# Six matmuls over zeros behind the weights' transposes, and one group of products moved, in a Winograd convolution

## The chip, the cores and the metric

The kernel runs on one core of a Trainium2 chip. The metric is the device time of one execution in microseconds (us); lower is better. Before the change three runs took 126.02 us in the median, from 125.92 to 126.29.

## The reference

```
batch, c_in, h, w, c_out = 16, 64, 64, 64, 128
x_pad = np.pad(x, ((0, 0), (0, 0), (1, 1), (1, 1)), mode='constant')
for b, co, ci, kh, kw:
    output[b, co] += weight[co, ci, kh, kw] * x_pad[b, ci, kh:kh+h, kw:kw+w]
```

It is a 3x3 convolution with zero padding of 16 images of 64 channels and 64x64 pixels to 128 channels, all in float32.

## The kernel before

The images are taken in eight pairs, p = 0 to 7. The 64 channels of two images fill the 128 partitions, so that a product of an image is a matmul over 64 rows, and the two images' matmuls stand side by side (`b2`). Each pair is worked in two halves of 32 output rows, h = 0 and 1: sixteen halves in all.

The convolution is done by Winograd's method along the rows of the image: two neighbouring output rows are made from sums, differences and outer differences of input rows with transformed weights (`G0`, `G1`, `G2`, `G01`, `G21`, and `HP` and `HM`, which are half sums). In each half, sixteen row pairs are split in two blocks of eight: the F block is done by Winograd, the G block by another way of combining. A half has four accumulators in PSUM: `pf1`, `pg1`, `pf2` and `pg2`.

**Weights.** They are loaded as they lie (`w_raw`), cast to float16 by POOL and ACT (lines 84 and 85), and transposed on TensorE by nine matmuls against an identity (line 101), three for each kernel row kh in the order 0, 2, 1. Each kernel row has a tile of two PSUM banks, of which the first bank is used. From these, ACT and DVE make the transformed weights (lines 147 to 158). DVE's string is `th` (149), `HP` (150), the first sums `ss` (112), `HM` (153), the first differences `dd` (119), `G01` (156), `G21` (158) and the first outer differences `ee` (130). `th` reads the transposes of kh = 2.

**The loop.** For each half, POOL prepares sums, differences and outer differences two halves ahead (line 230; DVE makes those of the very first half itself), and ACT casts a part of the input (line 140). TensorE then runs seven groups of products through `mms` (line 178), in the order of the text: `pf1` from sums with `HP`, `pg1` from sums with `G1`, `pf2` from differences with `HM`, `pg2` from the cast input with `G01` and `G2`, and then the second parts: `pf1` from outer differences (`ee`) with `G0`, `pg1` from the cast input, `pf2` from `ee` with `G2`. ACT copies the first parts out (lines 245, 247, 249), and DVE and ACT put the halves together (lines 260 to 263): `g1` from `pg2`, `f0` from `pf1`, `f1` from `pf2`, `g0` from `pg1`.

**Order.** `keep` holds nearly every instruction in the order in which it is written, on each engine. PSUM has room for four tiles of two banks; a half's tile takes the room of whichever tile was given back first.

**Memory and transfers.** Eleven slots of SBUF (`homes`) hold both inputs and outputs: an output takes the slot of an input that is no longer wanted (`X_HOME`, `O_HOME`). Slot 6 is a spare at the start and holds the weights' intermediate values. All loads are issued by SyncE at the start, on one queue: first the weights, then nine transfers of x. The stores follow on the same queue. The first two are issued in the half (2, 0), behind line 262: an upper half of an image of pair 2, and an image of pair 0:

```
        if (p, h) == (2, 0):
            store(2, 1, 0, 32)
            store(0, 0)
```

Of the kernel before, what the change touches and what calls it, by code (L numbers as in the profile page):

```python
# [8 lines left out]
F32 = mybir.dt.float32  # L9
F16 = mybir.dt.float16  # L10
# [5 lines left out]
def kernel(  # L16
# [12 lines left out]
    nc = tc.nc  # L29
    B, CI, H, W = x.shape  # L30
    CO = weight.shape[0]
# [4 lines left out]
    keep = tc.keep_in_program_order  # L36
# [4 lines left out]
    psum = ctx.enter_context(tc.tile_pool(name="psum", bufs=4, space=bass.MemoryType.PSUM))  # L41
# [13 lines left out]
    def out_homes(p):  # L55
        lo, hi = O_HOME[p]
        return homes[:, lo : hi + 1 : hi - lo, :, :]
# [4 lines left out]
    def spared(at, n):  # L62
        return spare[:, at : at + n]
# [4 lines left out]
    def load(p, cuts=((0, H),)):  # L68
        for lo, hi in cuts:
            keep(  # L70
                nc.sync.dma_start(
                    xs[p][:, lo:hi, :], x_rows[128 * p : 128 * p + 128, lo:hi, :]
                )
            )

    load(0, ((0, 34), (34, H)))
    for p in range(1, NP):
        load(p)

    ident = spared(1920, 64).bitcast(F16)  # L80
    make_identity(nc, ident)

# [4 lines left out]
    G0, G1, G2, G21, G01, HP, HM = range(7)  # L87
# [7 lines left out]

    wps = {}
    for kh in (1, 0, 2):
        wps[kh] = psum.tile([128, 2, 512], F32, tag="acc", name="wp")[:, 0, 0 : 3 * CO]
    for kh in (0, 2, 1):
        for k in range(3):  # L100
            keep(nc.tensor.matmul(wps[kh][:, k * CO : k * CO + CO], w16[:, :, 3 * kh + k :: 9], ident))  # L101


    F_BLK, G_BLK = (1, 2), (0, 3)
# [33 lines left out]
    def cast(p, h):  # L138
        t = cpool.tile([128, 17, W], F16, tag="xh", name="xh")
        keep(nc.scalar.copy(t, xs[p][:, C_ROW[h] : C_ROW[h] + 17, :]))  # L140
        return t

    def transforms(eng, p, h):
        return sums(eng, p, h), diffs(eng, p, h), outers(eng, p, h)
# [17 lines left out]
    def mms(tiles, terms, start, stop):  # L162
        n = 3 * len(terms)
        i = 0
        for wi, src, row in terms:
            for kw in (1, 0, 2):
                c_lo, c_hi = max(0, 1 - kw), min(W, W + 1 - kw)
                lo, hi = 0, RB
                at, step, rows = row
                while at + step * lo < 0:  # L170
                    lo += 1
                while at + step * (hi - 1) > rows - 1:
                    hi -= 1
                first, last = at + step * lo, at + step * (hi - 1)
                for b2 in range(2):
                    p0 = 64 * b2
                    keep(
                        nc.tensor.matmul(  # L178
                            tiles[:, b2, lo:hi, c_lo:c_hi],
                            Wt[p0 : p0 + 64, wi, kw, :],  # L180
                            src[
                                p0 : p0 + 64,
                                first : last + 1 : step,
                                c_lo + kw - 1 : c_hi + kw - 1,
                            ],
                            start=start and i == 0,
                            stop=stop and i == n - 1,
                            skip_group_check=not start,
                        )
                    )  # L190
                i += 1

    def acc():
        return psum.tile([128, 2, RB, W], F32, tag="acc", name="acc")
# [3 lines left out]
    def store(p, b2, lo=0, hi=H, c=0, n=CO, eng=nc.sync):  # L198
        keep(
            eng.dma_start(  # L200
                out[2 * p + b2, c : c + n, lo:hi, :], out_homes(p)[c : c + n, b2, lo:hi, :]
            )
        )
# [9 lines left out]
    def stores(p, h):  # L213
# [3 lines that stand above are left out]
        elif (p, h) == (2, 1):  # L217
            store(2, 1, 32, H)
            store(0, 1)
            store_both(1)  # L220
            store(2, 0)
        elif (p, h) == (5, 1):
            store(5, 0)
            store(5, 1, 0, FEW)
        elif p > 2 and h == 1:
            store_both(p)

    for n, (p, h) in enumerate(halves):
        if n + 2 < len(halves):
            tr[halves[n + 2]] = transforms(nc.gpsimd, *halves[n + 2])  # L230
        if h == 0:
            both = out_homes(p)
            ov = both.rearrange("p b (j i) c -> p b j i c", i=2)
        ss, dd, ee = tr.pop((p, h))
        xc = xh.pop((p, h))
        jf, jg = RB * F_BLK[h], RB * G_BLK[h]
        sf, sg = jf - 16 * h, jg - 16 * h
        g_at = 2 * jg - C_ROW[h]


        f0, f1 = (ov[:, :, jf : jf + RB, i, :] for i in range(2))
        g0, g1 = (ov[:, :, jg : jg + RB, i, :] for i in range(2))
        pf1, pg1, pf2, pg2 = acc(), acc(), acc(), acc()
        mms(pf1, [(HP, ss, (sf, 1, 16))], True, True)
        keep(nc.scalar.copy(f1, pf1))  # L245
        mms(pg1, [(G1, ss, (sg, 1, 16))], True, True)
        keep(nc.scalar.copy(g1, pg1))  # L247
        mms(pf2, [(HM, dd, (0, 1, RB))], True, True)
        keep(nc.scalar.copy(f0, pf2))  # L249
        if (p, h) == (6, 0):  # L250

            store(5, 1, FEW, H, 0, 124, nc.scalar)
            store(5, 1, FEW, H, 124, 4, nc.scalar)
        if n + 1 < len(halves):
            xh[halves[n + 1]] = cast(*halves[n + 1])
        mms(pg2, [(G01, xc, (g_at, 2, 17)), (G2, xc, (g_at + 2, 2, 17))], True, True)
        mms(pf1, [(G0, ee, (16 * h, 2, 32))], False, True)
        mms(pg1, [(G21, xc, (g_at + 1, 2, 17)), (G0, xc, (g_at - 1, 2, 17))], False, True)
        mms(pf2, [(G2, ee, (16 * h + 1, 2, 32))], False, True)
        keep(nc.vector.tensor_add(g1, pg2, g1))  # L260
        keep(nc.vector.tensor_add(f0, pf1, f0))  # L261
        keep(nc.vector.tensor_sub(f1, f1, pf2))  # L262
        keep(nc.scalar.copy(g0, pg1))  # L263
        stores(p, h)
# [30 lines left out]
```

## Time and profile before

| | |
|---|---|
| median of three runs | 126.02 us |
| the profiled execution's own time | 126.17 us |
| its span, first to last instruction | 124.3 us |
| DMA | 50.77 MB, 408 GB/s over the span |
| TensorE matmuls busy | 95.5 us (77%), 873 instructions |
| POOL busy | 90.6 us (73%) |
| ACT busy | 81.3 us (65%) |
| DVE busy | 63.6 us (51%) |
| queue q1 (SyncE): share of the 16 DMA engines' time | 95.9% |

A span is the time from the first to the last instruction of the profiled execution; the device time is a little longer. The busy time of an engine adds its instructions. Because matmuls overlap in the pipeline, a busy TensorE is not one at its peak: the distance between the starts of matmuls tells its pace. The slices of the profile cut the span in 40 equal parts, and each digit is a busy share in tenths. A timeline lists instructions as start, length, engine, line, operation, output<-input, shapes and count; in brackets stand the idle time before them and what ended it.

### The profile page before, as it was taken

The page shows a single profiled execution, that of the slowest core. Times are in us where ns is not written, and L with a number is a line of the kernel's source. Part 1 is how long each engine was busy: PE and PEld are TensorE (multiplying, and loading weights), DVE is VectorE, ACT ScalarE, POOL GpSimd, SP SyncE. Part 2 cuts the span into 40 slices and gives each one's busy share as a digit, 9 for nine tenths or more (in the row PEclk, how much of TensorE's full clock was granted, in tenths as well). Part 3 has the DMA queues.
Part 4 walks back from the last instruction along what each step waited for, and adds up shares of the span by engine and source line. Part 5 has one row for each costly group of instructions (what it writes and reads, how often), then busy time and mean ns, then how long its engine had stood idle before and what let it go on. Part 6 is the DMA issues. An engine that isn't in the chain of part 4 may idle for free.

```text
span 124.3 us, 2114 instructions
## 1 busy us (share of the span) xinstructions
PE 95.5 (77%) x873; PEld 49.8 (40%) x873; DVE 63.6 (51%) x56; ACT 81.3 (65%) x86; POOL 90.6 (73%) x52
## 2 busy tenths in 40 slices
PE   0329999999999998969999999999999996000000
PEld 0214555555455553534555555555555552000000
DVE  0099848393928472908294837556483939000000
ACT  4466798879697938659979797888888793000000
POOL 2209999999999999999999999999999700000000
PEclk9999999999999999999999999999999999655555
DMA  4999999999999999999999999999999999999980
GB/s 112 388 443 432 443 427 438 417 422 422 427 427 438 411 464 401 432 438 417 422 424 435 438 427 424 422 438 422 431 418 441 416 436 421 421 422 448 427 369 37
DMA packets 3954, 50.77 MB, mean 408 GB/s; under 512 B 360, under 2 KB 488, under 8 KB 744
## 3 DMA queue, kind: packets, MB, share of 16 engines
q1 hardware_dynamic: 3808, 50.40, 95.9%
q10 hardware_dynamic: 136, 0.23, 0.5%
q8 instruction: 7, 0.11, 0.3%
q14 instruction: 3, 0.02, 0.0%
HBM read 17.07 MB, written 33.55 MB: 407 GB/s over the span
## 4 chain that ended last, share of the span: by engine, by line
PE 68%; DMA 10%; DVE 4%; ACT 2%; POOL 1%; issue 0%; ACTq 0%; SPq 0%; DVEq 0%
PE acc L178 68%; DMA out_dram<-homes 7%; DMA homes<-in_weight_dram 3%; DVE homes L262 2%; DVE ss L112 1%; ACT homes L245 1%; ACT homes L247 1%; POOL homes L84 1%; DVE homes L149 0%; DVE Wt L150 0%; PE wp L101 0%; ACT homes L147 0%; ACTq L245 0%; SPq L200 0%; DVEq L150 0%
## 5 line engine op out<-in xcount | busy, mean ns | idle before, releaser
L178 PEld LDWEIGHTS <-Wt 64*128 64x128 f16 x864 | 48.8, 95 | 49.2 <-issue 5.3
L178 PE MATMUL acc<-xh,Wt 64*128 64x504 f16 (+3 forms) x384 | 45.9, 370 | 0.2
L112 POOL TENSOR_TENSOR ss<-homes 128x1024 f16<-128x1024 f32 x15 | 35.4, 2360 | 4.3 <-DMA homes<-in_x_dram 4.3
L260 DVE TENSOR_TENSOR homes<-acc,homes 128x1024 f32<-128x1024 f32 x16 | 19.6, 1224 | 34.9 <-PE acc L178 16.9
L130 POOL TENSOR_TENSOR ee<-homes 128x960 f16<-128x960 f32 (+1 forms) x15 | 35.3, 2350 | 0.0
L178 PE MATMUL acc<-ee,Wt 64*128 64x504 f16 (+1 forms) x192 | 26.5, 377 | 1.5 <-ACT homes L245 1.5
L178 PE MATMUL acc<-ss,Wt 64*128 64x504 f16 (+1 forms) x192 | 24.9, 392 | 2.3 <-DVE ss L112 2.3
L245 ACT COPY homes<-acc 128x1024 f32<-128x1024 f32 x16 | 16.2, 1012 | 10.1 <-DMA out_dram<-homes 4.6
L263 ACT COPY homes<-acc 128x1024 f32<-128x1024 f32 x16 | 16.3, 1017 | 8.5 <-PE acc L178 8.5
L262 DVE TENSOR_TENSOR homes<-homes,acc 128x1024 f32<-128x1024 f32 x16 | 19.5, 1219 | 1.0 <-PE acc L178 0.2
L119 POOL TENSOR_TENSOR dd<-homes 128x512 f16<-128x512 f32 x15 | 20.0, 1332 | 0.0
L261 DVE TENSOR_TENSOR homes<-acc,homes 128x1024 f32<-128x1024 f32 x16 | 19.4, 1214 | 0.0
L140 ACT CAST xh<-homes 128x1088 f16<-128x1088 f32 x16 | 17.9, 1118 | 0.1
L249 ACT COPY homes<-acc 128x1024 f32<-128x1024 f32 x16 | 16.5, 1030 | 0.0
L247 ACT COPY homes<-acc 128x1024 f32<-128x1024 f32 x16 | 16.3, 1017 | 0.3 <-PE acc L178 0.3
L178 PE MATMUL acc<-dd,Wt 64*128 64x504 f16 (+1 forms) x96 | 13.3, 379 | 0.0
L101 PE MATMUL wp<-homes 128*128 128x128 f16 x9 | 1.1, 312 | 5.1 <-POOL homes L84 5.1
L149 DVE SCALAR_TENSOR_TENSOR homes<-wp,homes 128x384 f32<-128x384 f32 x1 | 0.6, 558 | 6.1 <-ACT homes L147 6.1
L101 PEld LDWEIGHTS <-homes 128*128 128x128 f16 x9 | 0.9, 160 | 5.0 <-POOL homes L84 5.0
L84 POOL CAST homes<-homes 128x576 f16<-128x576 f32 x1 | 0.7, 662 | 3.0 <-DMA homes<-in_weight_dram 3.0
L130 DVE TENSOR_TENSOR ee<-homes 128x1088 f16<-128x1088 f32 x1 | 2.5, 2504 | 0.0
L85 ACT CAST homes<-homes 128x576 f16<-128x576 f32 x1 | 0.7, 671 | 2.3 <-DMA homes<-in_weight_dram 2.3
(17 smaller groups left out, 8.2 us busy)
## 6 DMA issues: line engine op xcount, KB each, us to landing
out_dram<-homes SPq DMA_DIRECT2D x5, 4096.0 KB, 21.2
homes<-in_x_dram SPq DMA_DIRECT2D x7, 2048.0 KB, 30.4
out_dram<-homes SPq DMA_DIRECT2D x4, 2048.0 KB, 16.6
out_dram<-homes SPq DMA_DIRECT2D x2, 1024.0 KB, 6.7
out_dram<-homes SPq DMA_DIRECT2D x1, 1824.0 KB, 20.8
homes<-in_x_dram SPq DMA_DIRECT2D x1, 1088.0 KB, 5.6
homes<-in_x_dram SPq DMA_DIRECT2D x1, 960.0 KB, 7.5
homes<-in_weight_dram SPq DMA_DIRECT2D x1, 288.0 KB, 3.5
```

Of the source, the lines that this page charges most:

```text
L112: keep(eng.tensor_add(t, v[:, j : j + 16, 0, :], v[:, j : j + 16, 1, :]))
L119: keep(eng.tensor_sub(t, v[:, j : j + RB, 1, :], v[:, j : j + RB, 0, :]))
L130: eng.tensor_sub(ees[p][:, lo - 16 : hi - 16, :], xs[p][:, lo - 1 : hi - 1, :], xs[p][:, lo + 1 : hi + 1, :],)
L140: keep(nc.scalar.copy(t, xs[p][:, C_ROW[h] : C_ROW[h] + 17, :]))
L178: nc.tensor.matmul(tiles[:, b2, lo:hi, c_lo:c_hi], Wt[p0 : p0 + 64, wi, kw, :], src[p0 : p0 + 64, first : last + 1 : step, c_lo + kw - 1 : ...
L245: keep(nc.scalar.copy(f1, pf1))
L247: keep(nc.scalar.copy(g1, pg1))
L249: keep(nc.scalar.copy(f0, pf2))
L260: keep(nc.vector.tensor_add(g1, pg2, g1))
L261: keep(nc.vector.tensor_add(f0, pf1, f0))
L262: keep(nc.vector.tensor_sub(f1, f1, pf2))
L263: keep(nc.scalar.copy(g0, pg1))
```

## The change

Three edits are made.

- A stretch of 256 float32 words of the spare slot is set to zero by DVE and read as 512 columns of float16 (`zeros`).
- Behind the nine transposes TensorE runs six matmuls whose stationary operand is 128 columns of the zeros and whose moving operand is all 512. Their result goes to the second bank of the last transposes' tile that the loop over (1, 0, 2) made, that of kh = 2. Nothing reads it.
- In the very first half (n = 0) the second part of `pg1` is written ahead of that of `pf1`, so that the products of the outer differences for `pf1` come last but one. In all other halves the order is as before.

```diff
+    zeros = spared(1984, 256).bitcast(F16)
+    keep(nc.vector.memset(zeros, 0.0))
     ident = spared(1920, 64).bitcast(F16)
...
     for kh in (1, 0, 2):
-        wps[kh] = psum.tile([128, 2, 512], F32, tag="acc", name="wp")[:, 0, 0 : 3 * CO]
+        wp = psum.tile([128, 2, 512], F32, tag="acc", name="wp")
+        wps[kh], idle_out = wp[:, 0, 0 : 3 * CO], wp[:, 1, :]
...
+    for _ in range(6):
+        keep(nc.tensor.matmul(idle_out, zeros[:, 0:CO], zeros, start=True, stop=True))
...
-        mms(pf1, [(G0, ee, (16 * h, 2, 32))], False, True)
-        mms(pg1, [(G21, xc, (g_at + 1, 2, 17)), (G0, xc, (g_at - 1, 2, 17))], False, True)
+        ends = [
+            (pf1, [(G0, ee, (16 * h, 2, 32))]),
+            (pg1, [(G21, xc, (g_at + 1, 2, 17)), (G0, xc, (g_at - 1, 2, 17))]),
+        ]
+
+        for tiles, terms in ends if n else ends[::-1]:
+            mms(tiles, terms, False, True)
```

## The prediction

> Lines are those of the kernel before. All times are us of the one profiled execution, whose span is 124.3 and whose own time is 126.17: 1.87 lie around the span. The three timed runs have 126.02 as their median, 0.15 below it, so what the change adds is put on 126.02. About 0.38 (0.3%) is the least that such a measurement can tell from no change.
>
> **What bounds the kernel now.** I read the slices of the page first.
>
> ```profile
> PEclk9999999999999999999999999999999999655555
> DMA  4999999999999999999999999999999999999980
> ```
>
> Each digit is 3.1 us. The DMA engines are busy from the second slice to the last but one, while TensorE stops at 104.5. The end is therefore that of 50.4 MB on one in-order queue (q1, SyncE's): what does not leave a hole in that queue costs nothing, and what makes TensorE faster gains nothing. So I looked for the place where the queue comes nearest to running dry. It is the first store, line 200, which waits for line 262 of the half (2, 0) (first fence from a window of DVE's timeline, second from SyncE's; start, length, engine).
>
> ```profile
> 38.85 1.22 DVE L262 TENSOR_TENSOR homes<-homes,acc 128x1024 f32<-128x1024 f32 x1
> ```
>
> ```profile
> 40.23 0.83 SPq L200 DMA_DIRECT2D out_dram<-homes  x2
> ```
>
> The packet records of the same trace say how near it is. The last load ends at 42.15 on the first of the 16 DMA engines, by 42.48 on ten of them, at 42.7 to 42.9 on four and at 44.0 on two; each goes straight on to the store's packets. The very first DMA (weights) was issued at 0.74 and its first packets began on the 16 engines at 1.76 to 2.09, 1.02 to 1.35 later. The same from 40.23 gives 41.25 to 41.58: the first engine is **0.6 to 0.9 from dry**. At all later stores the margin is larger: the one of 45.90 meets a queue full until 49.5, the last one (105.82) a queue full until 110.3.
>
> Next, what sets the time of that store. The chain of waits has TensorE without a pause from 8.55 to 44.6, so whatever the first half loses arrives at the store whole. The start, from the timeline:
>
> ```profile
> 5.08 1.15 PE L101 MATMUL wp<-homes 128*128 128x128 f16 x9 [5.08 <-POOL homes L84]
> 6.15 0.56 DVE L149 SCALAR_TENSOR_TENSOR homes<-wp,homes 128x384 f32<-128x384 f32 x1 [6.15 <-ACT homes L147]
> 6.81 0.56 DVE L150 SCALAR_TENSOR_TENSOR Wt<-wp,homes 128x384 f16<-128x384 f32 x1
> 7.28 1.22 DVE L112 TENSOR_TENSOR ss<-homes 128x1024 f16<-128x1024 f32 x1
> ...
> 8.55 2.75 PE L178 MATMUL acc<-ss,Wt 64*128 64x512 f16 x12 [2.32 <-DVE ss L112]
> ...
> 9.48 0.55 DVE L156 TENSOR_TENSOR Wt<-wp,Wt 128x384 f16<-128x384 f32 x1
> 9.95 0.55 DVE L158 TENSOR_TENSOR Wt<-wp,Wt 128x384 f16<-128x384 f32 x1
> ...
> 10.42 2.50 DVE L130 TENSOR_TENSOR ee<-homes 128x1088 f16<-128x1088 f32 x1
> ...
> 11.06 0.92 PE L178 MATMUL acc<-dd,Wt 64*128 64x512 f16 x6
> ...
> 13.11 0.82 PE L178 MATMUL acc<-ee,Wt 64*128 64x512 f16 x6
> ...
> 15.62 1.47 PE L178 MATMUL acc<-ss,Wt 64*128 64x512 f16 x12
> ```
>
> DVE runs one string: L149 (`th`), L150 (`HP`), L112 (`ss`), and the first product follows `ss` at 8.55. Between 6.2 and 8.55 TensorE is idle. The twelve products from 8.55 to 11.06 run as six pairs (two halves of the rows side by side), 0.42 a pair; the same twelve from 15.62 to 16.92 take 0.217 a pair. So the clock is at half until about 11.26; the PEclk column does not show that. At the end it does:
>
> ```profile
> 7.84:11.26 3.42, 2.71 (x14) 1.19 (x15) 3.42 (x6) 2.43 (x4) 1.96 (x1) 1.00 1.08 459
> ...
> 52.21:55.63 3.42, 2.27 (x24) 1.13 (x22) 0.35 (x1) 1.30 (x2) 3.42 (x3) 1.00 1.02 436
> 103.42:106.83 3.41, 1.08 (x10) 0.34 (x6) 2.27 (x2) 1.01 (x1) 0.00 (x0) 1.00 1.01 422
> 106.83:110.24 3.41, 0.00 (x0) 0.00 (x0) 0.00 (x0) 0.00 (x0) 0.00 (x0) 0.50 0.97 415
> ```
>
> (Busy us of PE, PEld, DVE, ACT, POOL, then PEclk, DMA share, GB/s.) The clock rose after 2.71 of work. It halved at 106.83, 2.3 after the last matmul, when the last 3.41 held 1.08 of work; the pause in 52.21 to 55.63, with 2.27 of work left, did not halve it.
>
> **The change part by part.**
>
> 1. The memset of the zeros is one DVE instruction ahead of L149, when DVE has nothing to do until 6.15. No memset of DVE is in the trace; the bounds are 0.20 (POOL's memset of 128x128) and 0.55 (L156). It is hidden by those 6 us; without that cover it would cost itself.
>
> 2. Six matmuls of 128x512, which before has not. At half clock one should take what a pair of 512 columns takes, 0.427 between starts (the transposes of 128 columns agree: 0.107 each); at full clock 0.217. The transposes are all issued by 6.02. All slow: issued by 8.58, the last result 0.2 later, 8.78. All fast: 7.49. The transposes and zeros are unbroken work from 5.08, and 2.71 of it brought the clock up before, so about at 7.8: then 4.2 of them are slow, and the end is 6.02 + 4.2 x 0.427 + 1.8 x 0.217 + 0.2 = 8.40. I take that (it goes by the rise in the trace).
>
> 3. **The wait.** The zeros' results go into the second bank of the tile whose first bank holds the transposes of kh = 2, and the built program treats it as one tile: `th` (L149), which waited for 6 matmuls, now waits for 15, the last of the zeros. It starts at 8.40 + 0.11 (matmul end to DVE start, as at L260) = 8.51 in place of 6.15. L150 has one wait less, -0.05. All of DVE's string behind it moves by 2.31: `HP`, `ss`, `HM`, dd, G01, G21, ee; ScalarE's G1, its cast and G2 wait for `HP` and move too, but are needed later. First product: 8.55 + 2.31 = **10.86**. (Bounds by 2: 9.95 to 11.24.)
>
> 4. **The clock.** The gap it opens is 8.40 to 10.86, 2.46, longer than the 2.3 after which the clock fell at the end, and the 3.41 before 10.86 hold 0.95 of work, less than the 1.08 there. So I take it to be at half again at 10.86 and up after 2.71 more of work, at 13.57, which costs 1.35. At full clock the half's products need (rows from 11.8 on) 1.30 + 0.65 + 1.30 + 1.21 + 0.65 + 0.65 = 5.76. The half ends at 10.86 + 5.76 + 1.35 = 17.97, against 15.62: 2.35 late. (Bounds: nothing; or, if the transposes count too, 3.86 of work before the rise, 1.93.)
>
> 5. The move of the ee products. Before, they start at 13.11 and ee is ready at 12.92, so at most 0.2 was waited for; the gain is at most that. After, ee is ready at 15.2, and TensorE reaches those products later, at 16.7: no wait. It has a price: L261 now comes behind the last but one group and L262 behind L261, ending some 2.75 after the last group's start (before 17.05 - 14.97 = 2.08). The second half's fourth group needs that bank at 2.60: 0.15 to 0.2 of stall. Together **2.5 late**. The bounds of 2 and 4 give 0.5 to 3.5. No instruction of POOL or SyncE moves; the 12 added of TensorE are 0.7% of its 1748.
>
> 6. The queue. First store 40.23 + 2.5 = 42.73, its packets from 43.75 to 44.08. The ten engines that were done by 42.48 stand still for about 1.6, the four for 1.1, the two for nothing. Each engine has its own fixed share of rows, so what it loses it does not get back. Does the last engine lose it? At the last landing it is 2.9 behind the first. The two that are 1.9 behind at 42.15 are still 1.87 and 1.89 behind at the landing of 90.80, where another is 2.98 behind. So the last is, as I read it, one of the ten. Sum: 126.02 + 1.6 = **127.6** (1.6 on the profile's 126.17 would be 127.8).
>
> The Trainium skill ("DMA: Bandwidth & Descriptors", Specifications) gives about 0.6 as the first-byte latency of such a DMA; the trace shows 1.02. By the page the hole is 0.4 smaller, and the time 127.2 in place of 127.6.
>
> **The rivals.**
>
> *The clock holds through the gap.* A pause of 1.15 did not halve it; between that and 2.3 nothing is shown. Then step 4 costs nothing, the half is late by 1.4 to 1.8 (zeros partly or all slow, G01 0.2 late included), the packets come at 42.8 to 43.2, and the hole is 0.5 to 0.9: 126.5 to 126.9. By the Trainium skill ("TensorE: Matmul & The Clock Gate", Part 1) the clock falls only after an idle window of some 3.4 us, which a gap of 2.46 need not hold; that speaks for this one. The end of the trace speaks against it: there the window before the fall held 1.08 of work.
>
> *Not slower: the margin swallows it.* If the clock is up by 6.8, the zeros end by 7.87, the first product comes by 10.33, the half is at most 0.9 late and the store's packets meet engines still loading: 126.0 to 126.2. Against it: the clock rose in this trace only after 2.7 of work, and by 6.8 there is 1.7.
>
> *The zeros do not count as work for the clock.* Then the zeros are all slow, the first product comes at 11.24 and the clock rises at 13.95: the half is 2.9 late, the hole 2.0, the time 128.0; by the bound of 3.5, 128.6. No row shows a matmul over zeros.
>
> A gain needs a hole that is there now, and between 3 and 119 the queue has none.
>
> **How the numbers follow.** Clock falls again 0.52 (127.1 to 128.1, predicted 127.6); zeros not counted 0.10 (127.6 to 128.6); clock holds 0.20 (126.5 to 126.9); margin swallows 0.15; something faster 0.03. The range from 126.3 to 128.6 leaves out the last two. Slower by over 0.3%, that is over 126.40: 0.52 + 0.10 + 0.17 = 0.79; same 0.15 + 0.03 = 0.18; faster 0.03.
>
> **What would show it.** `th` starting at 8.4 to 8.9 right behind the zeros (step 3); the first product at 10.8 to 11.3; its pairs at 0.42 again (step 4); first store at 42 to 43.2; a dip of the DMA row near 43 to 44; spans that grow by the hole. A store before 41.2 or a DMA row without a dip would make it wrong.

## The result and the profile after

The changed kernel takes **130.26 us** in the median of six runs (128.31 to 131.53), the kernel before 126.13 (125.92 to 126.46): slower, by a ratio of 1.0245 (95% interval 1.0205 to 1.0285). Every ratio in this text leaves out runs that are over 1.5% above the fastest of the same kernel, so this one goes by the runs at 128.31, 129.72 and 130.11. The profile shown is that of the run at 131.53, the longest of the six, with a span of 129.6, in which the clock came up late, as is told below. Direction and place are as forecast. The size is not: 127.6 was predicted, 128.6 was the upper end of the range.

From the page of the changed kernel, the slices (3.2 us each):

```profile
PEclk9998569999999999999999999999999999955555
DMA  4999999999999059999999999999999999999981
```

The clock row now has a dip near the start, and the DMA row has the hole that the prediction feared in its fourteenth slice. A finer look at it, from the windows of the changed kernel (us and busy us of PE, PEld, DVE, ACT, POOL, then PEclk, DMA share, GB/s):

```profile
43.00:44.00 1.00, 1.00 (x14) 0.57 (x12) 1.00 (x2) 0.43 (x2) 1.00 (x2) 1.00 0.08 33
44.00:45.00 1.00, 1.00 (x12) 0.54 (x10) 1.00 (x2) 0.98 (x1) 1.00 (x2) 1.00 0.00 0
45.00:46.00 1.00, 1.00 (x13) 0.55 (x10) 0.83 (x1) 0.66 (x1) 1.00 (x1) 1.00 0.00 0
```

The loads run out from 42.07 on (42.15 before), and nothing is left to move until the first store comes. SyncE's timeline gives it:

```profile
45.98 0.82 SPq L206 DMA_DIRECT2D out_dram<-homes  x2
```

It was issued at 40.23 before, so it is 5.75 late, not 2.5. Its first packets begin at 46.83. By the packet records the 16 DMA engines stand idle there for 4.3 in the mean (4.76 on the first that runs dry), and the span is 5.3 longer. The other 1.0 lies in the packets: those of q1, the same 50.40 MB, take 92.7% of 129.6 = 120.1 after and 95.9% of 124.3 = 119.2 before. TensorE (first column) is busy all the while: the lost time lies in the queue, but its cause lies further ahead. The start, from the timeline of the changed kernel:

```profile
5.71 2.72 PE L107 MATMUL wp<-homes 128*128 128x512 f16 x6
...
8.55 0.56 DVE L155 SCALAR_TENSOR_TENSOR homes<-wp,homes 128x384 f32<-128x384 f32 x1 [7.42 <-PE wp L107]
...
9.20 2.34 POOL L118 TENSOR_TENSOR ss<-homes 128x1024 f16<-128x1024 f32 x1 [4.55 <-DMA homes<-in_x_dram]
9.61 3.01 DVE L118 TENSOR_TENSOR ss<-homes 128x1024 f16<-128x1024 f32 x1
...
12.68 2.74 PE L184 MATMUL acc<-ss,Wt 64*128 64x512 f16 x12 [4.24 <-DVE ss L118]
...
13.01 1.29 DVE L125 TENSOR_TENSOR dd<-homes 128x512 f16<-128x512 f32 x1
...
21.28 1.04 PE L184 MATMUL acc<-ss,Wt 64*128 64x512 f16 x8
```

`th` (now L155) waits for the zeros, as forecast, and starts at 8.55 (8.51 predicted). What differs comes two instructions later: DVE's `ss` takes 3.01 where it took 1.22. POOL's sums for a later half had begun at 9.20 and ended at 11.54; DVE's instruction started at 9.61 and ended 1.08 behind POOL's. DVE looks busy, but, as the experiments will show, it stands still until POOL is through, and then does its work. So the first product comes at 12.68 and not at 10.86. (The last line is the start of the second half's products: 15.62 before.)

And the clock, in windows of the changed kernel between the records of its changes (PE alone, then PEclk):

```profile
8.26:11.67 3.41, 0.17 (x1) 1.00 0.99 423
11.67:15.09 3.42, 2.42 (x12) 0.50 1.04 446
15.09:18.50 3.41, 3.41 (x18) 0.50 0.99 423
```

It rose at 8.26, fell at 11.67 after a stretch with 0.17 of work, and rose again only at 18.50: a stretch with 2.42 of work did not bring it up. Before, one with 2.71 did.

### The profile page after: what moved, and what is told of

Read it like the earlier page. It is cut to its first block, busy times and chain, and to the rows that moved or that the text cites. A ratio compares the mean times of both kernels' runs of the same rounds, so it can differ in the third digit from the quotient of the medians.

```text
span 129.6 us, 2127 instructions
## 1 busy us (share of the span) xinstructions
PE 99.3 (77%) x879; PEld 51.7 (40%) x879; DVE 66.3 (51%) x57; ACT 81.5 (63%) x86; POOL 91.8 (71%) x52
## 3 DMA queue, kind: packets, MB, share of 16 engines
q1 hardware_dynamic: 3808, 50.40, 92.7%
## 4 chain that ended last, share of the span: by engine, by line
PE 76%; DVE 4%; DMA 2%; ACT 1%; POOL 1%; issue 0%; DVEq 0%
PE acc L184 73%; DMA homes<-in_weight_dram 2%; DVE ss L118 2%; PE wp L107 2%; DVE homes L273 1%; PE wp L104 1%; ACT homes L251 1%; ACT homes L253 1%; POOL homes L86 1%; DVE homes L155 0%; DVE Wt L156 0%; DVEq L155 0%
## 5 line engine op out<-in xcount | busy, mean ns | idle before, releaser
L184 PEld LDWEIGHTS <-Wt 64*128 64x128 f16 x864 | 50.0, 96 | 51.4 <-issue 8.5
L184 PE MATMUL acc<-xh,Wt 64*128 64x504 f16 (+3 forms) x384 | 46.8, 376 | 0.1
L118 POOL TENSOR_TENSOR ss<-homes 128x1024 f16<-128x1024 f32 x15 | 36.7, 2444 | 4.6 <-DMA homes<-in_x_dram 4.6
L136 POOL TENSOR_TENSOR ee<-homes 128x960 f16<-128x960 f32 (+1 forms) x15 | 36.1, 2404 | 0.0
L184 PE MATMUL acc<-dd,Wt 64*128 64x504 f16 (+1 forms) x96 | 13.9, 392 | 0.0
L155 DVE SCALAR_TENSOR_TENSOR homes<-wp,homes 128x384 f32<-128x384 f32 x1 | 0.6, 558 | 7.4 <-PE wp L107 7.4
L118 DVE TENSOR_TENSOR ss<-homes 128x1024 f16<-128x1024 f32 x1 | 3.0, 3009 | 0.0
L157 ACT CAST Wt<-wp 128x384 f16<-128x384 f32 x1 | 0.5, 479 | 3.6 <-DVE Wt L156 3.6
L107 PE MATMUL wp<-homes 128*128 128x512 f16 x6 | 2.7, 624 | 0.0
```

The costliest lines, as they stand in the source:

```text
L118: keep(eng.tensor_add(t, v[:, j : j + 16, 0, :], v[:, j : j + 16, 1, :]))
L136: eng.tensor_sub(ees[p][:, lo - 16 : hi - 16, :], xs[p][:, lo - 1 : hi - 1, :], xs[p][:, lo + 1 : hi + 1, :],)
L184: nc.tensor.matmul(tiles[:, b2, lo:hi, c_lo:c_hi], Wt[p0 : p0 + 64, wi, kw, :], src[p0 : p0 + 64, first : last + 1 : step, c_lo + kw - 1 : ...
```

## The experiments

The theory after the result: **the wait of `th` moves DVE's string beside POOL's sums, DVE stands still there, the first half ends late, and the queue runs dry in front of the first store.** The rivals: the clock alone makes it (it falls in the gap); the zeros themselves cost TensorE time; the moved group costs; the loss comes later than the first store and not through the queue. "First store" below is the time of its issue in the profiled execution.

### The parts by themselves

**The zeros alone:** the changed kernel with the old order of the groups.

```diff
-        for tiles, terms in ends if n else ends[::-1]:
+        for tiles, terms in ends:
```

> The zeros alone; all groups of products in the old order. Queue theory (the time is that of before plus what SyncE's queue stands still in front of the first store; the first half is late by the wait for the zeros, by DVE's sums lying beside POOL's, and by the clock): as with the whole change, first store near 45 to 46, 128.3 to 131.5. Rival, the moved group is what costs: 126.1.

Measured: 129.88 (129.65 to 130.38), ratio 1.0267 (1.0233 to 1.0301). `ss` starts at 9.45 and takes 3.21, the first product comes at 12.72, the first store at 44.75. The whole loss is there without the moved group.

**The moved group alone:** the kernel before, with the new order in the first half.

> The moved group alone, no zeros. Queue theory: the half gains at most 0.2 and loses at most 0.2, the first store stays within 0.3 of 40.23, inside the margin of 0.6 to 0.9: 126.1 (125.8 to 126.4). Rival, the moved group is what costs: 128 or more.

Measured: 126.07 (125.84 to 126.69), ratio 0.9968 (0.9949 to 0.9986). Since that interval leaves out 1 by a hair, the same kernel ran once more in more rounds:

> The moved group alone once more, in five rounds: it read 0.3% below before. Queue theory: no hole in either, 126.1 to 126.4, within 0.3% of before. Rival, the new order is worth something: 0.3% or more below before again.

Measured: 126.33 (126.01 to 126.99), ratio 1.0008 (0.9990 to 1.0026), first store at 40.17. The move alone is worth nothing that shows. (The first of the two profiled runs, the longest of its ten, had its first store at 41.46, outside the 0.3 that was expected: there the clock rose at 14.07, in the second at 11.50.)

**The zeros without the wait:** their results go to a fourth PSUM tile, which nothing reads, so `th` waits for the transposes alone.

```diff
+    idle_out = psum.tile([128, 2, 512], F32, tag="acc", name="wq")[:, 1, :]
     for _ in range(6):
```

> The six zeros write to the fourth PSUM tile, which no other engine reads, so the DVE instruction th waits for the transposes alone. Queue theory: th back at 6.15, ss at 7.28 for 1.22, first product near 8.6, first store at or before 40.3, no hole: 126.1. Rival, the zeros cost something as such (TensorE's time, the clock), whoever waits for them: 128 to 131.

Measured: 126.22 (125.96 to 127.51), ratio 0.9998 (0.9967 to 1.0030). `th` starts at 5.51. The same six matmuls run, and the loss is gone: it is the wait and not the matmuls. (The clock still fell at 11.07 and rose at 14.49.) The profiled run, at 127.25 one of the slower of its ten, got its first x late, `ss` waiting for a DMA until 8.76, and its first store was at 42.19.

**Two zeros in place of six.**

> Two zeros in place of six, same tile and same wait. th is 0.7 late (two slow matmuls), ss still ends before POOL begins at 9.2 to 9.3, first store some 0.7 late: at the edge of the margin of 0.6 to 0.9. Queue theory: 126.1 to 126.5. Rival, TensorE's lateness goes to the end in any case: 126.8; rival, the cost goes by the number of zeros (a third of 4.1): 127.5.

Measured: 126.78 (126.25 to 129.48), ratio 1.0010 (0.9975 to 1.0045). `th` starts at 6.44, `ss` at 7.51, ahead of POOL's sums, and takes 1.21; the first product is at 8.77. Counted from the first transpose, `th` starts 1.05 later than before (2.12 in place of 1.07), but `ss` comes ahead of POOL's 9.30 and keeps its length. In this profiled run the first store comes 1.22 later than before and the span is 0.5 longer, so most of the lateness is swallowed; the forecast for lateness that goes to the end in any case, 126.8, lies too near to be told apart by the times. Three of the ten runs took 128.80 to 129.48. There is no profile of them, and what made them late stays open, so that two zeros are harmless in seven runs only (126.25 to 127.18).

### Does DVE stand still beside POOL?

**POOL beside DVE, without any zeros:** the kernel before, with one addition on POOL into spare words, over the same data that DVE's `ss` reads.

```diff
...
+    keep(nc.gpsimd.tensor_add(beside, v0[:, 0:16, 0, :], v0[:, 0:16, 1, :]))
```

> The kernel before, no zeros, with one more tensor_add of 128x1024 on POOL, into spare words that nothing reads, from about 6.5 to 8.9, beside DVE's ss (7.28 before). Theory that DVE's sum of two SBUF inputs stands still while POOL's sum runs: ss ends near 10 in place of 8.5, dd waits for POOL's next sum and ends near 12.3, the first half is about 2 late, first store 41.5 to 42.7, a hole of 0.3 to 1.5: 126.4 to 127.8. Rival, the 3.0 us of ss in the changed kernel came from the zeros or the clock: ss takes 1.22, 126.1.

Measured: 128.40 (127.47 to 128.58), ratio 1.0137 (1.0091 to 1.0184). From its timeline:

```profile
6.80 2.35 POOL L149 TENSOR_TENSOR homes<-homes 128x1024 f16<-128x1024 f32 x1 [2.17 <-DMA homes<-in_x_dram]
6.95 3.27 DVE L112 TENSOR_TENSOR ss<-homes 128x1024 f16<-128x1024 f32 x1
9.12 3.31 POOL L112 TENSOR_TENSOR ss<-homes 128x1024 f16<-128x1024 f32 x1
10.15 0.55 DVE L156 SCALAR_TENSOR_TENSOR Wt<-wp,homes 128x384 f16<-128x384 f32 x1
...
10.62 2.37 DVE L119 TENSOR_TENSOR dd<-homes 128x512 f16<-128x512 f32 x1
```

DVE's `ss` ends 1.07 behind POOL's 9.15, as in the changed kernel (1.08), although it began only 0.15 behind POOL. Then it is POOL's turn to stand: its next sums take 3.31 in place of 2.35, 0.96 more, about what DVE still had to do. So the two take turns, instruction by instruction, and whoever came first finishes first. The line at 10.15, which reads PSUM and SBUF, keeps its 0.55 beside POOL. The price was above what was expected: the first store went to 43.30, as `dd` behind it was held up too (2.37 in place of 0.68), and the clock rose at 15.04 (11.26 before).

The Trainium skill ("SBUF — State Buffer", Who interferes with whom) states this: a DVE instruction with two SBUF inputs contends with a GpSimd instruction that reads SBUF, and the one that issues later is blocked for the whole of the other. These rows agree with it, for either engine as the one that is blocked, to within 0.15: DVE needs 1.07 behind POOL's end, and 1.22 alone.

**POOL behind DVE, with the zeros:** the changed kernel, in which POOL first copies one column of DVE's `dd`, so that its sums wait until `ss` and `dd` are done.

```diff
...
+    keep(nc.gpsimd.tensor_copy(held, d0[:, 0, 0:1]))
     tr[0, 1] = transforms(nc.gpsimd, 0, 1)
```

> The whole change, but POOL's first sum waits, through a one-column copy, until DVE's dd is done, so that DVE's ss and dd have SBUF to themselves. Theory of standing still: ss takes 1.22 again, first product near 10.9 in place of 12.7, about 1.8 of the 5.7 goes: first store 42.7 to 44.5, 127.2 to 129.5. Rival, the length of ss has another cause: first product at 12.7, 128.3 to 131.5.

Measured: 128.03 (127.39 to 128.60), ratio 1.0122 (1.0068 to 1.0175). From its timeline:

```profile
9.50 1.21 DVE L118 TENSOR_TENSOR ss<-homes 128x1024 f16<-128x1024 f32 x1
...
10.77 1.90 PE L186 MATMUL acc<-ss,Wt 64*128 64x512 f16 x12 [2.46 <-DVE ss L118]
...
11.99 2.35 POOL L118 TENSOR_TENSOR ss<-homes 128x1024 f16<-128x1024 f32 x1
```

This is the only run with the whole wait in which neither `ss` nor `dd` stands still, and it comes out close to the numbers on record: first product 10.77 (10.86 predicted), end of the half 18.20 (17.97), first store 42.91 (42.73), time 128.03 (127.6). The end of the half is near partly by luck: the clock was still up at 10.77, fell at 11.68 and rose at 15.09, where it was predicted at half from 10.86 to 13.57. Against the zeros alone, 129.88, the standing still is worth 1.85.

### The clock

**The gap filled:** the changed kernel with twenty more matmuls over zeros, in a tile of their own, so that TensorE works until the first products.

```diff
...
+    for _ in range(20):
+        keep(nc.tensor.matmul(more_out, zeros[:, 0:CO], zeros, start=True, stop=True))
```

> The whole change with 20 more zeros, in the fourth PSUM tile, that nobody waits for but TensorE: they fill its gap up to the first product, so the clock should stay up. First product near 13.2 (it waits for one more DVE instruction). Theory that half of the lateness is the clock: the first half's products run at 0.217 a pair, the half ends near 19.3 to 19.5 in place of 21.3, first store near 44, 128.0 to 129.2. Rival, the clock plays no part: 129.5 to 131.5 as the whole change.

Measured: 129.94 (129.77 to 130.15), ratio 1.0298 (1.0266 to 1.0331): a miss, as more was expected of it. The clock came up at 8.92 and stayed up, yet the half ended at 19.99, beside 20.15 with the zeros alone, where the clock fell at 12.12 and rose at 15.54. This does not isolate the clock, since the added tile brings waits of its own: the first product comes at 13.21 (12.72 with the zeros alone), and the second group then waits 0.85 for DVE's `G01` (L165 there). What can be read is this. With the zeros alone the products of `ee` start at 17.63, right behind the end of DVE's `ee` (15.20 + 2.38 = 17.58): there DVE's string sets the end of the half, and the clock adds little.

In the changed kernel the `ee` products come later in the order, and the clock does count. The run with one store ahead, below, has the same start, and its first product comes at 12.66. Its clock rose at 15.46 and the half ended at 19.78. In the profiled run of the changed kernel the clock rose at 18.50 and the half ended at 21.28, 1.5 later.

### The queue

**A late store and nothing else:** the kernel before, with the first two stores moved behind the next half and behind the store that was third; the work at the start is untouched.

```diff
-        if (p, h) == (2, 0):
+        if (p, h) == (2, 1):
+            store(2, 1, 32, H)
             store(2, 1, 0, 32)
             store(0, 0)
-        elif (p, h) == (2, 1):
-            store(2, 1, 32, H)
```

> The kernel before, without zeros; only the first three stores are issued in another order, so that the first one issued is the one whose data are ready last, at 45.9. Nothing of the compute at the start is touched. Queue theory: the queue stands still from 42.1 (44.0 on the last two engines) to 46.7, as in the changed kernel: 130.5 (129.5 to 131). Rival, the loss is TensorE's lateness and not the queue's: TensorE is not late here, 126.1.

Measured: 131.36 (130.96 to 132.04), ratio 1.0392 (1.0346 to 1.0438). By chance its first store is issued at 45.98 too, as in the changed kernel, and the span is 129.3 beside 129.6, though the first product came at 8.07. From its windows:

```profile
44.00:45.00 1.00, 1.00 (x12) 0.54 (x10) 0.86 (x2) 0.97 (x1) 1.00 (x1) 1.00 0.00 0
45.00:46.00 1.00, 1.00 (x14) 0.47 (x11) 0.90 (x1) 0.04 (x1) 1.00 (x2) 1.00 0.09 16
```

It is the same hole (4.0 in the mean by the packet records, 4.3 in the changed kernel), with TensorE as busy. (In this kernel a pause of TensorE in the middle let the clock fall once more, which the changed kernel does not have.) A late store by itself makes a loss of this size; nothing of the start need be late for it.

**One store ahead of the tight place:** the changed kernel, in which `store(0, 0)`, 2 MB, is issued already in the half (0, 1).

```diff
-        if (p, h) == (2, 0):
+        if (p, h) == (0, 1):
+            store(0, 0)
+        elif (p, h) == (2, 0):
             store(2, 1, 0, 32)
-            store(0, 0)
```

> The whole change, but the store of image 0 (2 MB, ready near 32) is issued ahead of the first one and stands behind the loads in the queue. The first half is as late as before this edit. Queue theory: the queue has 4.9 us more in it when the other stores come at 44 to 46, and has no hole or one under 0.5: 126.1 to 126.8. Rival, TensorE's lateness goes to the end in any case: 129 to 131.

Measured: 128.72 (127.79 to 128.94), ratio 1.0163 (1.0117 to 1.0209): a miss. In the profiled run, at 127.79 the shortest of the four, the hole is smaller, not gone; the other three took 128.61 to 128.94 and have no profile. It has moved behind the next store (windows of this kernel):

```profile
49.00:50.00 1.00, 1.00 (x14) 0.51 (x10) 1.00 (x1) 0.23 (x1) 1.00 (x2) 1.00 1.05 434
50.00:51.00 1.00, 1.00 (x12) 0.51 (x10) 0.08 (x1) 0.00 (x0) 1.00 (x2) 1.00 0.22 90
```

What was drawn ahead of the loads' end is missing behind the store of 44.48, and the one of 50.15 comes too late. **The same in the kernel before**, to see whether it helps there:

> The kernel before with the store of image 0 issued ahead of the others, no zeros. Queue theory: the queue has no hole now, so none is filled: 126.1, within 0.3%. Rival, single executions of before have small holes at the first store, which this closes: 125.9 and a narrower spread than 125.9 to 126.5.

Measured: 126.80 (126.30 to 127.63), ratio 1.0052 (1.0031 to 1.0073): slower by half a per cent, against what was expected. With that store ahead of them, the transfers behind it land later, and slots of SBUF come free later: the last store is issued at 112.22 (105.82 before), and the queue is short of work there: the DMA share from 112 to 113 is 0.44.

**Two stores ahead:** the changed kernel with `store(0, 1)` drawn forward as well.

> The whole change with both stores of pair 0 (4 MB) issued ahead of the first store. With one of them ahead (2 MB) a hole stayed at 50.0 to 51.0, because the queue then held too little in front of the second half's store. Queue theory: with 9.8 us more behind the loads there is no hole before 56; the half (3, 0) waits longer for its slot, to about 56.5, so the last store comes near 111 and may leave a hole of 0 to 1.3 on the engines that are ahead: 126.2 to 127.4, below the 128.7 of one store ahead. Rival, TensorE's lateness goes to the end in any case: 128.7 or more.

Measured: 131.15 (130.69 to 131.41), ratio 1.0381 (1.0353 to 1.0410): a plain miss. There is no hole before 56, but one line of ACT shows what took its place:

```profile
57.74 1.01 ACT L252 COPY homes<-acc 128x1024 f32<-128x1024 f32 x1 [8.98 <-DMA out_dram<-homes]
```

An output of the half (3, 0) goes into a slot that a store must first leave. That store has landed only at 57.7, TensorE waits 7.2 for this copy, and the later stores of the pairs come late instead. No version was found that beats the kernel before.

The start of this run shows something else, by chance. Up to there its instructions are those of the changed kernel, but the order of two of them is the other way round:

```profile
9.31 1.22 DVE L118 TENSOR_TENSOR ss<-homes 128x1024 f16<-128x1024 f32 x1
9.39 3.34 POOL L118 TENSOR_TENSOR ss<-homes 128x1024 f16<-128x1024 f32 x1 [5.10 <-DMA homes<-in_x_dram]
10.58 2.75 PE L184 MATMUL acc<-ss,Wt 64*128 64x512 f16 x12 [2.46 <-DVE ss L118]
```

DVE's `ss` came 0.08 ahead of POOL's, and it was POOL that stood still. So at the place to which the change moves the string, a few tenths decide who waits: POOL's sums start when a load lands (9.2 to 9.4), and DVE's `ss` when the zeros are through (9.3 to 9.7). In the profiled runs of the changed kernel, of the zeros alone, of the filled gap and of the one store ahead, POOL came first.

### All runs on one line

| kernel | first store, us | span, us | 124.3 + (first store - 40.23 - 0.7) |
|---|---|---|---|
| before | 40.23 | 124.3 | in time |
| the move, again | 40.17 | 124.4 | in time |
| two zeros | 41.45 | 124.8 | 124.8 |
| the move | 41.46 | 124.9 | 124.8 |
| zeros in their own tile | 42.19 | 125.5 | 125.6 |
| zeros, POOL behind DVE | 42.91 | 126.2 | 126.3 |
| POOL beside DVE | 43.30 | 126.7 | 126.7 |
| gap filled | 44.69 | 128.0 | 128.1 |
| zeros alone | 44.75 | 128.1 | 128.1 |
| late store | 45.98 | 129.3 | 129.4 |
| after | 45.98 | 129.6 | 129.4 |

The rows take in every kernel with the stores in their old order, and the late store. The span of each profiled execution follows the time of its first store to within 0.3, whatever made the store late. The margin of 0.7 is fitted to the rows; 0.6 to 0.9 was on record.

This is a fit, and not all of what it fits is standing still. In the rows at 41.45 and 41.46 the packet records show less than 0.1 of added idle time in the mean, yet the packets of q1 take 96.2% of 124.8 = 120.1 and 96.1% of 124.9 = 120.0, in place of 119.2. In all rows from 41.45 on they take 120.0 to 120.4. Why the same bytes take some 0.8 to 1.2 longer there stays open.

## Why the prediction was right in direction and wrong in size

- **What bounds it.** Right. The queue is the bound and the first store its tight place; the late store alone makes a loss of this size, and the spans of the table rise as its first stores do, behind the margin.
- **Steps 1 and 2.** Right. The memset does not show on the path, and the six matmuls ended where `th` could start at 8.55 (8.51). They were nearly all slow, 0.427 apart; the clock rose at 8.26, when the last was almost done. (If all were fast, the terms of step 2 give 7.52 and not 7.49; nothing hangs on it.)
- **Step 3, the wait.** Right in what it waits for: with its own tile the loss is gone, and with two zeros it is gone in seven runs of ten. **The step that failed is its next sentence, "All of DVE's string behind it moves by 2.31"**: it moved the string with the durations of its old place. In its new place `ss` lies beside POOL's sums, and took 3.01 in place of 1.22; `dd` took 1.29 in place of 0.68. The bounds of the step, 9.95 to 11.24 for the first product, asked only when the string starts; the measured 12.68 lies outside. The sign was in the trace of before: `ee`, shown as 2.50 long, ended at 12.92, 1.15 behind the end of POOL's sums, which were not looked at:

```profile
9.30 2.47 POOL L112 TENSOR_TENSOR ss<-homes 128x1024 f16<-128x1024 f32 x1 [4.35 <-DMA homes<-in_x_dram]
```

  The prediction's own `ss` would have begun at 7.28 + 2.31 = 9.59, 0.29 behind this line. The 2.50 was read as the price of `ee`, not as that of its company.
- **Step 4, the clock.** Right that the clock is lost, but not through a gap of 2.46: in the changed kernel the gap was 4.2 (8.43 to 12.68). A gap of the predicted length is that of POOL behind DVE, 8.32 to 10.77. There the clock held through the gap and fell at 11.68, at the end of a stretch with 0.95 of work. Mis-sized in the rise: "after 2.71 more of work" was taken as an amount, counted from the first product. The records show stretches of 3.41 with fixed ends, and the work within one either is enough or is not. In the profiled run the first product came in the midst of one, and the clock rose at 18.50, not 13.57: from the first product to the end of the half it took 8.60, 2.84 more than the 5.76 of full speed, where 1.35 was put. Where the stretches end differs from run to run. That, and who comes first of DVE and POOL, I take to be what spreads the runs of the changed kernel. It is argued, since only one of them has a profile; but the three profiled kernels with this start ended the half at 21.28 (after), 19.78 (one store ahead) and 19.31 (two stores ahead, where DVE came first).
- **Step 5, the moved group.** 0.15 to 0.2 was put; nothing shows within 0.3%. With DVE's `ee` late, the move does shorten the half: 20.15 with the zeros alone, 19.78 with the move (one store ahead), the clock having risen at 15.54 and 15.46.
- **Step 6, the queue.** Right in kind, and near in number partly by luck: 2.5 late was to cost 1.6, and by the table it costs 1.8. With POOL behind DVE the store was 2.68 late, the engines stood still for 1.1 in the mean, and the span grew by 1.9; the rest is the longer time of the packets, which the prediction put at nothing. The packets began 0.85 behind the issue, where 1.02 was taken. The first-byte latency of the Trainium skill ("DMA: Bandwidth & Descriptors", Specifications), 0.6, is short of both.
- **The rivals.** The clock holds: in the changed kernel and with POOL behind DVE it was down for most of the first products (fallen at 11.67 and 11.68), though in the second it had held through the gap itself. The margin swallows it: the store came 5.75 late. The zeros do not count as work: the clock rose at 8.26, at the end of a stretch filled by the transposes and them, and in the filled gap it stayed up on zeros alone. The rival that was missing is the one that came: that DVE's string meets POOL.
- **The signs.** `th` at 8.55, the first products at half speed and the dip of the DMA row came as listed. The first product (12.68) and the first store (45.98) did not.

The sum with the missing term: 126.02 + 1.6 + 1.85 (the zeros alone less POOL behind DVE) = 129.5, beside 129.72, the median of the three runs that the ratio goes by, and 129.88 for the zeros alone. In the profiled run the first store was 45.98 - 42.73 = 3.25 later than predicted: 12.68 - 10.86 = 1.82 by the first product, 2.84 - 1.35 = 1.49 by the clock, and 0.06 less by the rest.

## What to carry to other kernels

When a wait moves a string of instructions, look up in the trace what the other engines do at the string's new place, and price its instructions beside that: a duration belongs to a place, not to an instruction. Work that is only there to keep an engine warm must not share a tile with anything that is waited for. In this kernel, whose queue is full from end to end, one time, that of the transfer with the least margin, went with the whole to within 0.3, and drawing transfers forward moved the tight place rather than removed it.

## What the runs showed of the hardware that was not expected

- DVE additions with both inputs in SBUF and POOL additions did not share time but took turns, by whole instructions: 1.22 became 3.00 to 3.27, ending 1.07 to 1.09 behind POOL's end, and POOL's 2.35 became 3.31 and 3.34 when it came second. DVE instructions with one input in PSUM kept their 0.55 beside POOL.
- The clock goes by stretches of 3.41 whose ends do not depend on the work: within a run its changes lie multiples of 3.41 apart (8.26, 11.67, 18.50 after; 8.71, 12.12, 15.54 with the zeros alone), and from run to run they lie elsewhere. Stretches with 2.39 (two stores ahead), 2.42 (after) and 2.61 (the move) of work did not raise it; 2.67 (the store of image 0 ahead in the kernel before), 2.71 (before), 2.82 and 2.93 (zeros alone, POOL beside DVE) did. Once up, it stayed up with 2.45 (filled gap), 2.27 (before) and even 1.50 (two stores ahead, 50.10 to 53.52), and fell with 1.41 (one store ahead, 107.62 to 111.04), 1.34 (own tile) and less. The Trainium skill ("TensorE: Matmul & The Clock Gate", Part 1) has such a free-running window, and these rows agree; but its rule that an idle window precedes the fall does not hold for the stretches with 1.41 and 1.34.
- Matmuls over zeros hold the clock up: in the filled gap it stayed at full from 8.92 on, through a stretch (8.92 to 12.33) that they alone filled.
